# A decayed cumulative sum of a matmul: 210 of 264 slots ordered by a list scheduler, solved in place in a ring of seven tiles

## The chip, the cores and the metric

The kernel runs on one core of one Trainium2 chip. The metric is device microseconds of one execution. Engines are named as the profile names them: PE (TensorE matmul), PEld (its weight loads), DVE (VectorE), ACT (ScalarE), POOL (GpSimd), SP (SyncE, which here only issues stores).

## The reference

```python
B, S, D = 16, 2048, 1024
xw = x @ w                                    # x: [B, S, D], w: [D, D]
out[:, 0, :] = xw[:, 0, :]
for t in range(1, S):
    out[:, t, :] = decay[None, :] * out[:, t - 1, :] + xw[:, t, :]
```

Inputs and output are float32 in HBM. The kernel multiplies in bf16 and adds up in float32.

## The kernel before, in words

**Chunks and slots.** The 16 x 2048 rows of x are cut into 64 chunks of 512 rows. Two chunks of one batch entry are a group. For a group and one of eight blocks of 128 output columns PE makes one product of 128 columns by 1024 time steps, in a PSUM tile `ps` of which there are three. This is a *slot*: 16 matmuls of 128x512. There are 264 slots; the last group's two chunks are taken one at a time, in slots of half the size. Slot s of the middle of the kernel works on group s // 8, that is chunks 2(s // 8) and 2(s // 8) + 1, and on column block n = s % 8.

**How x comes in.** A chunk is loaded as four quads by POOL's DMA queue (`load`, letter L) into one of three `xb` tiles; DVE transposes it (`turn`, T) into one of two `xw` tiles; ACT copies it in two halves (`part`, X and Y) into one of five `xt` tiles, from which PE reads.

**How a slot is solved.** Most slots are *paired*. ACT copies the product to a tile `xs` (`copy`, p) and multiplies its even places by the decay into a tile `h` (`odd`, g); POOL adds these to the odd places (`join`, j); DVE scans only the odd places with the squared decay (`scan`, S) into a tile `so`; ACT multiplies the result by the decay again (`even`, h); POOL adds it to the even places (`fill`, c). ACT also copies the value before the first place (`zero`, z; POOL clears it at the start of a batch entry) and keeps the last one for the next group (`save`, k). A slot that is not paired is scanned whole by DVE, straight from PSUM. DVE then transposes `so` back (`back`, B) into an output tile `ot`. Four slots fill one `ot`, a *lump*; then SP issues four stores of 512 KB. Before, there are four `ot`, four `so`, three `xs`, four `h`. Of four slots three are paired, with a few exceptions listed in `flips`.

**What a release is.** PE may begin slot s when ACT (p and g) or, for a slot that is not paired, DVE (S) is done with `ps` of slot s - 3. A `so` is free again after its B, an `ot` after its four stores have landed, an `xt` after the last slot of its group, an `xb` after its T.

**What sets the order.** `pin` keeps each engine's instructions in the order in which the kernel's code issues them; an engine runs its list from the front, and an instruction that waits holds up what stands behind it. The text `agenda` gives the order slot by slot for slots 0 to 33 and for the last 20; for the slots between, `usual(s)` issues P, S, C, B in a fixed pattern, and `later` places each T, X and Y a fixed number of slots ahead of the group that needs it (11, 10 and 8 slots for an even chunk, 7, 6 and 4 for an odd one); one quad is loaded per slot.

In the built program the loads of x take eight semaphores in turn, and each load first waits until the load eight before it has landed.

Of the kernel before, what the change touches and what calls it, by code (L numbers as in the profile page):

```python
# [25 lines left out]
def kernel(  # L26
# [26 lines left out]
    nc = tc.nc  # L53
# [13 lines left out]
    CH = D // 2  # L67
    CR = CH // NQ

    const = ctx.enter_context(tc.tile_pool(name="const", bufs=1))  # L70
# [23 lines left out]
    def ot_tile(nj):  # L94
        return ring(sb, "ot", 4, [128, nj, CR])

# [22 lines left out]
    def part(c, copy, m0, m1, j0=0, j1=NJ):  # L119
        if c not in xt_of:  # L120
            xt_of[c] = ring(sb, "xt", 5, [128, M, 2, TL], BF16)
        src = xw_of[c][:, m0:m1, j0:j1].rearrange("p m j i e -> p m e (j i)")
        pin(copy(out=xt_of[c][:, m0:m1, :, j0 * P:j1 * P], in_=src))  # L123
# [17 lines left out]
    class Tile:  # L141
# [3 lines left out]
        def __init__(self, g, n, ps, outlets):  # L145
            self.b, self.t0 = chunks[g[0]]
            self.T = TL * len(g)
            self.n, self.ps, self.outlets = n, ps, outlets
            self.paired = n % R != R - 1
            if len(tiles) in flips or len(tiles) - len(slots) in flips:  # L150
                self.paired = not self.paired
            self.turn = len(tiles)
            self.lot = sum(t.paired for t in tiles)
            self.prev = None if self.t0 == 0 else last[n]
            if self.t0 + self.T < S:
                last[n] = const.tile([128, 1], FP32, name=f"keep{n}", bufs=2)
                self.keep = last[n]
            else:
                self.keep = None

        @property
        def so(self):
            if not hasattr(self, "held"):
                self.held = sb.tile([128, 2 * TL + 2], FP32, name=f"so{self.turn % 4}")
            return self.held

        def decayed(self, src):
            h = ring(sb, "h", 4, [128, TL])[:, 0:self.T // 2]
            pin(nc.scalar.activation(  # L169
                out=h, in_=src, func=mybir.ActivationFunctionType.Copy,  # L170
                scale=dec[:, self.n:self.n + 1]))
            return h
# [8 lines left out]
        def copy(self):  # L181
            self.xs = sb.tile([128, 2 * TL], FP32, name=f"xs{self.lot % 3}")[:, 0:self.T]
            pin(nc.scalar.copy(out=self.xs, in_=self.ps))  # L183

        def odd(self):
            self.g = self.decayed(self.ps[:, 0:self.T:2])

        def zero(self):
            if self.prev is None:
                pin(nc.gpsimd.memset(self.so[:, 1:2], 0.0))  # L190
# [3 lines left out]
        def join(self):  # L194
            odds = self.xs[:, 1:self.T:2]
            pin(nc.gpsimd.tensor_tensor(out=odds, in0=self.g, in1=odds, op=ALU.add))  # L196

        def scan(self):
            T, n, so = self.T, self.n, self.so
            if self.paired:  # L200
                pin(nc.vector.tensor_tensor_scan(  # L201
                    out=so[:, 3:T + 2:2],
                    data0=squares[-1][:, n:n + 1].to_broadcast([128, T // 2]),
                    data1=self.xs[:, 1:T:2],
                    initial=0.0 if self.prev is None else self.prev,
                    op0=ALU.mult,
# [8 lines left out]
        def run(self, ps, t, size):  # L215
# [3 lines left out]
            else:  # L219
                before = 0.0 if self.prev is None else self.prev  # L220
            pin(nc.vector.tensor_tensor_scan(  # L221
# [12 lines left out]
        def complete(self):  # L234
            if self.paired:
                self.even()
                self.fill()
            if self.keep is not None:
                self.save()

        def even(self):
            self.h = self.decayed(self.so[:, 1:self.T + 1:2])

        def fill(self):
            T = self.T
            pin(nc.gpsimd.tensor_tensor(  # L246
                out=self.so[:, 2:T + 2:2], in0=self.h, in1=self.xs[:, 0:T:2], op=ALU.add))

        def save(self):
            pin(nc.scalar.copy(out=self.keep, in_=self.so[:, self.T + 1:self.T + 2]))  # L250

# [14 lines left out]
    class Outlet:  # L266


        def __init__(self, ns, nj, half=0, queues=(nc.sync,), pieces=1):
            self.pieces = pieces  # L270
            self.ns, self.missing, self.half = ns, set(ns), half
            self.nj, self.t0, self.queues = nj, half * nj * P, queues
            self.ot = ot_tile(nj)

# [133 lines left out]
    def turn_and_load(c):  # L408
# [60 lines left out]
        20: "Y7 S19 L c16 k17 h17 T8 k19 L c17",  # L469
        21: "p20 g20 L S18 X8 j20 B17 B19",  # L470
        22: "L h18 p21 c18 B16 k18 g21 B18 Y8 z20 L j21 S20",
        23: "p22 z21 z22 S21 L h20 g22 T9 c20 h21",
        24: "k21 k20 j22 S23 X9 L c21 Y9 B20 L",
        25: "B23 k23 p24 B21 g24 z24 j24 S22 z25",
        26: "p25 T10 k22 h22 g25 c22 S24 X10 j25",
        27: "B22 p26 S25 g26 z26 Y10 j26",
        28: "S27 h25 h24 c25 S26 c24",
# [26 lines left out]
    flips = (1, 13, 15, -19, -18, -11, -8, -6, -3, -2)  # L504
    later = {}
    begun = {"T": 12, "X": 11, "Y": 11}
    for c in range(5, nch):
        first = c // 2 * K
        ahead = (7, 6, 4) if c % 2 else (11, 10, 8)
        for letter, a in zip("TXY", ahead):  # L510
            if c >= begun[letter]:
                later.setdefault(first - a, []).append(f"{letter}{c}")

    def usual(s):
        paired = [t.paired for t in tiles]
        do = [f"P{s}"] if paired[s] else []
        if paired[s - 1]:
            do.append(f"S{s - 1}")
        if not paired[s]:
            do.append(f"S{s}")  # L520
        do.append(f"C{s - 1}")
        if paired[s - 2]:
            do.append(f"B{s - 2}")
        if not paired[s - 1]:
            do.append(f"B{s - 1}")
        return do + later.get(s, []) + ["L"] * (2 if len(loads) > NQ else 1)

    def rest(s):
        do = [f"S{s - 1}"] if tiles[s - 1].paired else []
        do.append(f"C{s - 1}")  # L530
        if tiles[s - 2].paired:
            do.append(f"B{s - 2}")
        return do + [f"B{s - 1}"] + later.get(s, []) + ["L"] * len(loads)

    def perform(do):
        for deed in do:
            deeds[deed[0]](int(deed[1:] or 0))

    perform(agenda[-99].split())
    spares = [spare] + [ring(psp, "spare1", 1, [128, TL])]  # L540
    for step, (g, n) in enumerate(slots):
        T = TL * len(g)
        left = step - len(slots)
        if n % R == 0:
            ns, nj = range(n, n + R), T // P
            both = -6 * R <= left < -2 * R
            outlets = [Outlet(ns, nj, queues=(nc.sync, nc.gpsimd) if both else (nc.sync,),
                              pieces=2 if left == -2 * R else 1)]
        if left == -R:
# [52 lines left out]
        tiles.append(Tile(g, n, ps, outlets))  # L602
        do = agenda.get(step, agenda.get(left) if left >= -20 else None)
        if do is None:
            do = usual(step)
        else:
            do = do.split()
            if left == -20:
                do = rest(step) + do
        perform(do)  # L610
    assert not loads
# [28 lines left out]
```

## Time and profile before

| | us |
|---|---|
| Median of 3 runs (908.7 to 909.01) | 908.76 |
| Span of the profiled execution, first to last instruction | 907.2 |
| PE busy | 892.8 |
| DVE busy | 826.3 |
| ACT busy | 686.2 |
| POOL busy | 663.0 |

The profiled execution's own span is 907.2 us; the timed runs have 1.6 us more around it. Busy times count what overlaps on one engine once. PE's share cannot tell by itself whether PE could go faster, because its matmuls are pipelined and their ends are modelled; its list of waits and the number of weight loads in a stretch (one to a matmul) can. The trace lacks a few matmul records and the landing times of some stores.

### The profile page before, as it was taken

How to read it: one execution, taken by the hardware profiler on the slowest of the kernel's cores; microseconds unless marked ns; L12 is line 12 of the kernel's file. 1: busy time of each engine (PE TensorE's matmuls, PEld its weight loads, DVE VectorE, ACT ScalarE, POOL GpSimd, SP SyncE). 2: the span in 40 equal slices, each digit the busy share in tenths (PEclk: the TensorE clock that was granted, in tenths of full speed). 3: DMA queues.
4: the chain of work that ended last, by engine and by line, in shares of the span. 5: the costliest groups of instructions: out<-in, count | busy, mean ns of one | idle time of the engine just before them, and what ended most of it. 6: DMA issues, size and time to landing. Idle time of an engine off the chain costs nothing.

```text
span 907.2 us, 12004 instructions
## 1 busy us (share of the span) xinstructions
PE 892.8 (98%) x4119; PEld 411.4 (45%) x4201; DVE 826.3 (91%) x628; ACT 686.2 (76%) x955; POOL 663.0 (73%) x763
## 2 busy tenths in 40 slices
PE   9999999999999999999999999999999999999996
PEld 5444444444444444444444444444444444444443
DVE  4999989999999999899999999999999999999996
ACT  4889867777777877877877778778778778777742
POOL 7888678877777767768677777777677686776562
PEclk9999999999999999999999999999999999999999
DMA  9999999999999999999999999999999999999788
GB/s 194 194 215 220 227 215 220 215 238 255 249 250 254 241 243 259 247 244 228 227 233 227 227 232 227 226 232 233 220 230 231 228 231 223 232 229 207 153 161 211
DMA packets 397230, 204.77 MB, mean 226 GB/s; under 512 B 8816, under 2 KB 395376, under 8 KB 397168
## 3 DMA queue, kind: packets, MB, share of 16 engines
q1 hardware_dynamic: 258960, 131.62, 59.6%
q0 software_dynamic: 137920, 71.85, 58.1%
q8 instruction: 33, 0.54, 0.2%
q10 hardware_dynamic: 288, 0.52, 0.2%
q14 instruction: 29, 0.24, 0.1%
HBM read 138.42 MB, written 134.22 MB: 301 GB/s over the span
## 4 chain that ended last, share of the span: by engine, by line
PE 93%; DMA 2%; POOL 1%; issue 1%; DVE 1%; ACT 0%; POOLq 0%; DVEq 0%
PE ps L131 93%; DMA xb<-in_x_dram 2%; POOL ot L299 1%; POOL xb L105 1%; PE spare L131 1%; DVE xw L115 0%; ACT xt L123 0%; ACT xs L183 0%; DVE so L201 0%; PE spare L387 0%; DVE ot L258 0%; ACT h L169 0%; PE ps L387 0%; POOLq L635 0%; POOL xs L196 0%
## 5 line engine op out<-in xcount | busy, mean ns | idle before, releaser
L131 PE MATMUL ps<-xt,wsb 128*128 128x512 bf16 x3942 | 863.5, 378 | 4.7 <-ACT h L169 0.2
L131 PEld LDWEIGHTS <-wsb 128*128 128x128 bf16 x4152 | 405.9, 98 | 479.9 <-ACT wsb L306 0.8
L196 POOL TENSOR_TENSOR xs<-h,xs 128x512 f32<-128x512 f32 (+1 forms) x190 | 243.0, 1279 | 181.8 <-ACT h L169 79.4
L183 ACT COPY xs<-ps 128x1024 f32<-128x1024 f32 (+1 forms) x190 | 189.4, 997 | 155.3 <-PE ps L131 144.2
L258 DVE STREAM_TRANSPOSE ot<-so 128x1024 f32<-128x1024 f32 (+1 forms) x260 | 300.1, 1191 | 2.1 <-POOL so L190 1.1
L246 POOL TENSOR_TENSOR so<-h,xs 128x512 f32<-128x512 f32 (+1 forms) x190 | 241.4, 1272 | 39.0 <-ACT h L169 25.7
L123 ACT COPY xt<-xw 128x2048 bf16<-128x2048 bf16 (+1 forms) x136 | 242.3, 1790 | 7.8 <-DVE xw L115 7.6
L105 POOL DMA_DIRECT2D xb<-in_x_dram x264 | 174.3, 661 | 3.3 <-DMA ot<-in_w_dram 1.1
L169 ACT ACTIVATE h<-so,dec 128x512 f32<-128x512 f32 (+1 forms) x190 | 145.4, 766 | 27.7 <-DVE so L201 24.4
L115 DVE STREAM_TRANSPOSE xw<-xb 128x2048 f32<-128x2048 f32 (+1 forms) x78 | 147.4, 1901 | 5.5 <-DMA xb<-in_x_dram 5.5
L201 DVE TENSOR_TENSOR_SCAN so<-spare,keep,xs 128x512 f32<-128x512 f32 (+1 forms) x97 | 120.0, 1239 | 27.7 <-POOL xs L196 27.4
L201 DVE TENSOR_TENSOR_SCAN so<-spare,xs 128x512 f32<-128x512 f32 x93 | 113.3, 1220 | 27.6 <-POOL xs L196 24.6
L169 ACT ACTIVATE h<-ps,dec 128x512 f32<-128x512 f32 (+1 forms) x190 | 130.3, 686 | 0.0
L221 DVE TENSOR_TENSOR_SCAN so<-dec,ps 128x1024 f32<-128x1024 f32 x34 | 76.8, 2261 | 1.0 <-ACT h L169 1.0
L221 DVE TENSOR_TENSOR_SCAN so<-dec,keep,ps 128x1024 f32<-128x1024 f32 (+1 forms) x35 | 75.9, 2169 | 0.1
L250 ACT COPY keep<-so 128x1 f32<-128x1 f32 x136 | 25.3, 189 | 9.9 <-DVE so L221 9.4
L192 ACT COPY so<-keep 128x1 f32<-128x1 f32 x97 | 18.4, 191 | 2.6 <-DVE ot L258 2.4
L131 PE MATMUL ps<-xw,wsb 128*128 128x256 bf16 (+1 forms) x68 | 11.2, 301 | 0.1
L190 POOL MEMSET so<- 128x1 f32 x93 | 10.7, 117 | 0.6 <-DVE ot L258 0.6
L131 PE MATMUL spare<-xt,wsb 128*128 128x512 bf16 (+1 forms) x48 | 10.0, 335 | 0.0
L282 POOL DMA_DIRECT2D out_dram<-ot x8 | 5.7, 722 | 5.5 <-DVE ot L258 5.1
L299 POOL DMA_DIRECT2D ot<-in_w_dram x12 | 6.6, 546 | 3.3 <-DMA xb<-in_x_dram 2.0
(38 smaller groups left out, 44.5 us busy)
## 6 DMA issues: line engine op xcount, KB each, us to landing
out_dram<-ot SPq DMA_DIRECT2D x244, 512.0 KB, 10.9
xb<-in_x_dram POOLq DMA_DIRECT2D x248, 256.0 KB, 7.8
xb<-in_x_dram POOLq DMA_DIRECT2D x16, 128.0 KB, 5.8
out_dram<-ot POOLq DMA_DIRECT2D x4, 512.0 KB, 11.6
ot<-in_w_dram POOLq DMA_DIRECT2D x12, 128.0 KB, 5.1
out_dram<-ot SPq DMA_DIRECT2D x4, 256.0 KB
out_dram<-ot POOLq DMA_DIRECT2D x4, 256.0 KB, 8.5
out_dram<-ot SPq DMA_DIRECT2D x8, 128.0 KB, 4.3
```

The costliest lines, as they stand in the source:

```text
L105: pin(nc.gpsimd.dma_start(out=xb_of[c][quad(q), j0:j1], in_=_ap(x, [[D, P], [P * D, j1 - j0], [1, CQ]], (b * S + t0 + j0 * P) * D + q * CQ)))
L115: pin(nc.vector.transpose(out=dst.rearrange("p (m j i) -> p j m i", m=M, i=P)[:, j0:j1, m0:m1], in_=src.rearrange("p (j m c) -> p j m c", ...
L123: pin(copy(out=xt_of[c][:, m0:m1, :, j0 * P:j1 * P], in_=src))
L131: pin(nc.tensor.matmul(out=ps[:, t0:t1] if ps.shape[1] >= t1 else ps, lhsT=lhs, rhs=rhs, start=(k == 0 and t0 == start), stop=(k == K - 1),))
L169: pin(nc.scalar.activation(out=h, in_=src, func=mybir.ActivationFunctionType.Copy, scale=dec[:, self.n:self.n + 1]))
L183: pin(nc.scalar.copy(out=self.xs, in_=self.ps))
L196: pin(nc.gpsimd.tensor_tensor(out=odds, in0=self.g, in1=odds, op=ALU.add))
L201: pin(nc.vector.tensor_tensor_scan(out=so[:, 3:T + 2:2], data0=squares[-1][:, n:n + 1].to_broadcast([128, T // 2]), data1=self.xs[:, 1:T:2 ...
L221: pin(nc.vector.tensor_tensor_scan(out=so[:, t + 2:t + 2 + size], data0=dec[:, n:n + 1].to_broadcast([128, size]), data1=ps, initial=befor ...
L246: pin(nc.gpsimd.tensor_tensor(out=self.so[:, 2:T + 2:2], in0=self.h, in1=self.xs[:, 0:T:2], op=ALU.add))
L250: pin(nc.scalar.copy(out=self.keep, in_=self.so[:, self.T + 1:self.T + 2]))
L258: pin(nc.vector.transpose(out=outlet.ot[:, :, c0:c0 + P], in_=self.so[:, 2 + t0:2 + t0 + nj * P].rearrange("p (i t) -> p i t", t=P)))
```

## The change

The change replaces `usual` and `later`. For slots 34 to 243 a list scheduler in the kernel (`steady`, `in_order`) makes a job of each instruction, or of four matmuls for PE, with an engine, a cost in us, a due time (`key`) and the jobs that it comes after. It steps through time; an engine that is idle takes the ready job with the earliest due time, whatever that due time is. The order in which jobs start is the order in which they are issued. A load is assumed landed 9 us after its end (`LAND`), a store 13 us after the lump's last B (`STORED`). Chunks 12 to 14 have some or all of their quads loaded by the agenda; only quads still to be loaded become jobs.

Beside that:

- a product is copied straight into its `so` and solved there in place; `xs` is gone, and `so` has seven tiles, taken in turn at the copy;
- `ot` has three tiles instead of four, `xt` four instead of five; an `ot` is now taken when its first B is issued;
- which slots are not paired in 34 to 243 is set by a running sum (0.18 to a slot): 37 of 210, where it was 53;
- T is issued in two halves there;
- in the agenda X8 and Y8 move from slots 21 and 22 to 24, X9 and Y9 from 24 to 25 and 26, and X10 and Y10 leave it for the scheduler;
- code that merges the products of a group (`mixed_group`, `differ` and others) is added, but `merged` is empty and none of it runs.

```diff
+    OTS, XTS, SOS, HS = 3, 4, 7, 4
+    FROM, TO = 34, 244
+    SHARE = {-1: 0.08, 0: 0, 1: 0.12, 2: 0.16, 3: 0.18, 9: 0.18}
+    merged = ()
...
-        return ring(sb, "ot", 4, [128, nj, CR])
+        return ring(sb, "ot", OTS, [128, nj, CR])
...
-            xt_of[c] = ring(sb, "xt", 5, [128, M, 2, TL], BF16)
+            xt_of[c] = ring(sb, "xt", XTS, [128, M, 2, TL], BF16)
...
-                self.held = sb.tile([128, 2 * TL + 2], FP32, name=f"so{self.turn % 4}")
+                self.held = sb.tile([128, 2 * TL + 2], FP32, name=f"so{self.turn % SOS}")
...
         def copy(self):
-            self.xs = sb.tile([128, 2 * TL], FP32, name=f"xs{self.lot % 3}")[:, 0:self.T]
-            pin(nc.scalar.copy(out=self.xs, in_=self.ps))
+            pin(nc.scalar.copy(out=self.line, in_=self.ps))
...
         def join(self):
-            odds = self.xs[:, 1:self.T:2]
+            odds = self.line[:, 1:self.T:2]
             pin(nc.gpsimd.tensor_tensor(out=odds, in0=self.g, in1=odds, op=ALU.add))
...
-        21: "p20 g20 L S18 X8 j20 B17 B19",
-        22: "L h18 p21 c18 B16 k18 g21 B18 Y8 z20 L j21 S20",
+        21: "p20 g20 L S18 j20 B17 B19",
+        22: "L h18 p21 c18 B16 k18 g21 B18 z20 L j21 S20",
         23: "p22 z21 z22 S21 L h20 g22 T9 c20 h21",
-        24: "k21 k20 j22 S23 X9 L c21 Y9 B20 L",
-        25: "B23 k23 p24 B21 g24 z24 j24 S22 z25",
-        26: "p25 T10 k22 h22 g25 c22 S24 X10 j25",
-        27: "B22 p26 S25 g26 z26 Y10 j26",
+        24: "X8 k21 k20 j22 S23 Y8 L c21 B20 L",
+        25: "B23 k23 p24 B21 g24 z24 j24 S22 X9 z25",
+        26: "p25 T10 k22 h22 g25 c22 Y9 S24 j25",
+        27: "B22 p26 S25 g26 z26 j26",
...
+    def in_order():
...
+            for e, queue in ready.items():
+                if idle[e] > now:
+                    continue
...
+                job = heapq.heappop(queue)[2] if queue else None
...
+                order.append(job)
+                job.start = now
+                end = idle[e] = now + job.cost
...
+                for other, delay in next_to[job]:
+                    begin[other] = max(begin[other], end + delay + (GAP if other.engine != e else 0))
...
+    LAND = 9.0
+    STORED = 13.0
+    PASS = 0.2158
...
+        def chunk(c):
+            need = starts[c // 2] - 18 + (c % 2) * 5
+            if c > 11:
+                quads = [q for cc, q in loads if cc == c] if c <= 14 else range(NQ)
+                got = [Job("pool", cost["L"], need - 28 + 2.5 * q, lambda c=c, q=q: load(c, q),
+                           [turned.get(c - 3)]) for q in quads]
+                ends = [(a, LAND) for a in got]
+                for half in range(2):
+                    turned[c] = Job(
+                        "dve", cost["T"], need + 2 * half,
+                        lambda c=c, h=half: turn(c, 0, NJ, h * M // 2, (h + 1) * M // 2),
+                        ends + [turned.get(c - 1), part_of.get((c - 2, 1)), turned.get(c)])
+                    part_of[c, half] = Job(
+                        "act", cost["X"], need + 3 + 3 * half,
+                        lambda c=c, h=half: part(c, nc.scalar.copy, h * M // 2, (h + 1) * M // 2),
+                        [turned[c], part_of.get((c - 1, half))] + used.get(c - XTS, []))
...
+        def back(tile, end, key):
+            s = tile.turn
+            lump = s // R
+            first = firsts.get(lump - 1)
+            b = Job("dve", cost["B"], key + 6, tile.back,
+                    [end, place.get((s, "k"))] + stored.get(lump - OTS, []) + ([first] if first else []))
+            firsts.setdefault(lump, b)
+            place[s, "B"] = b
+            lumps.setdefault(lump, []).append((b, STORED))
+            if len(lumps[lump]) == R:
+                stored[lump] = lumps[lump]
...
+        order = in_order()
+        for job in order:
+            job.do()
...
     for step, (g, n) in enumerate(slots):
+        if FROM <= step < TO:
+            if step == FROM:
+                steady(outlets)
+            continue
...
-        do = agenda.get(step, agenda.get(left) if left >= -20 else None)
-        if do is None:
-            do = usual(step)
-        else:
-            do = do.split()
-            if left == -20:
-                do = rest(step) + do
-        perform(do)
+        perform(agenda.get(step, agenda.get(left)).split())
```

In the built program the first instructions of the scheduler's part stand like this (a number is the slot or the chunk, a small letter an instruction of a slot, as above). DVE: S33, B32, B33, both halves of T12, S34, S35, B34, S36, T13, B35, T13, B36, S37, S38, S39. POOL: the four L13, the first L14, c33, three L14, z34, j34, two L15, z35, one L15, j35, c34, z36, j36, one L15, c35. ACT: X10, k33, h33, X10, p34, g34, X11, p35, g35, h34, k34, p36, g36, X11, h35, k35, p37, h36, k36, g37. Slot 39 is not paired. The agenda's last loads, all four of chunk 12, stand two behind j32 and two behind c32 on POOL, before as after.

## The prediction

> **What bounds the kernel now.** I read the page first: its busy shares and its chain that ended last.
>
> ```profile
> span 907.2 us, 12004 instructions
> ...
> PE 892.8 (98%) x4119; PEld 411.4 (45%) x4201; DVE 826.3 (91%) x628; ACT 686.2 (76%) x955; POOL 663.0 (73%) x763
> ...
> PE ps L131 93%; DMA xb<-in_x_dram 2%; POOL ot L299 1%; POOL xb L105 1%; PE spare L131 1%; DVE xw L115 0%; ACT xt L123 0%; ACT xs L183 0%; DVE so L201 0%; PE spare L387 0%; DVE ot L258 0%; ACT h L169 0%; PE ps L387 0%; POOLq L635 0%; POOL xs L196 0%
> ```
>
> The chain is PE. Whether PE has gaps is told by its list of waits and by busy time in stretches of the middle.
>
> ```profile
> PE ps L131 <- ACT h L169: 0.2, 1, 0.2
> ...
> 200.00:300.00 100.00, 99.53 (x456) 45.33 (x464) 92.64 (x65) 77.52 (x106) 74.35 (x81) 1.00 1.23 251
> ```
>
> PE waits for another engine's `ps` release once, 0.2 us. In 100 us there are 464 weight loads, one to a matmul: 0.2155 us each, 3.45 us a slot, at a clock of 1.00. So PE runs without a gap through the slots that the change touches. The matmuls stay what they are, so this middle cannot become faster; the question is whether the new order keeps PE fed. Next I read who is close to being late: DVE around slot 34, the loads that it waits for, and the stores.
>
> ```profile
> 130.15 1.01 ACT L183 COPY xs<-ps 128x1024 f32<-128x1024 f32 x1 [1.09 <-PE ps L131]
> 134.58 1.30 POOL L105 DMA_DIRECT2D xb<-in_x_dram  x2
> 145.72 2.31 DVE L115 STREAM_TRANSPOSE xw<-xb 128x2048 f32<-128x2048 f32 x1 [0.56 <-DMA xb<-in_x_dram]
> ```
>
> From the timelines of ACT, POOL and DVE. The copy at 130.15 is that of slot 33, so slot 34 begins at 130.1 and slot s at 130.1 + 3.45 (s - 34). The last two quads of chunk 12 are issued at 134.6 and 135.2, and T12 waits for them until 145.7. That costs nothing now: it stands behind all that is due sooner.
>
> ```profile
> L282 SPq DMA_DIRECT2D out_dram<-ot x4: 4670/4723/4727, 156.9 to 171.1; - x4
> ...
> DMA to landing us min/median/max: 18.1/18.3/18.4
> ...
> L258 DVE STREAM_TRANSPOSE ot<-so x4: 1203/1212/1246, 134.7 to 142.9; 128x1024 f32<-128x1024 f32 x4
> L258 DVE STREAM_TRANSPOSE ot<-so x1: 1247/1247/1247, 175.9 to 175.9; 128x1024 f32<-128x1024 f32 x1
> L258 DVE STREAM_TRANSPOSE ot<-so x1: 1247/1247/1247, 189.7 to 189.7; 128x1024 f32<-128x1024 f32 x1
> ```
>
> From the instructions of `out_dram` and of line 258. 32 stores and 32 B precede, so these are lump 8 (slots 32 to 35): B done at 144.1, stores issued only from 156.9, the last landed at 171.1 + 18.4 = 189.5. The stores queue. With four `ot`, lump 12 takes this tile, first B at 189.7: 0.2 us to spare. Lump 11 begins at 175.9.
>
> **The change part by part.**
>
> *More paired slots.* 53 unpaired become 37, so 16 slots move. Rows by form: ACT p 1.012, g 0.694, h 0.775 and half a z of 0.19; POOL j 1.299, c 1.292; DVE one scan of 1.25 for one of 2.29. ACT gains 16 x 2.58 = 41 us, POOL 16 x 2.59 = 41, DVE loses 16 x 1.04 = 17. T in halves: a transpose of 128x1024 is 1.216, two are 0.15 more than the 2.285 of the whole, 52 times 8 us. Over the 725 us of the 210 slots busy shares go from 92 to 91% (DVE), 78 to 84 (ACT), 75 to 80 (POOL). None passes PE's 100: no cost by load, and DVE, which is nearest, gets a little looser. If a stall elsewhere makes DVE late, this cover is thin: it recovers some 9% of the time that passes.
>
> *Seven `so`, no `xs`, in place.* Same operations, sizes and strides; p now waits for the B of seven slots before (24 us) where it waited for a c of three paired slots before. No row shows a loss; 0, between -0.4 (below, last rival) and 0.
>
> *Four `xt`.* X may begin when the group before last ends, 27.6 us ahead; X8 to Y9 move to slots 24 to 26, needed at slot 32, at least 15 us ahead by the order. 0; ACT, which waits for chunk 8's place, does 3.8 us less in slots 21 and 22 and as much more in 24 to 26.
>
> *T12's place.* The scheduler has no load job for chunk 12, since the agenda issued them, so T12 counts as ready when X10 is done. DVE, idle until S34, takes it although it is due later. On the chip DVE runs its list in order and blocks on T12 till the data is there. First stall, slot 39, which needs slot 36's `ps`, released by g36, behind h34 and p36 on ACT:
> T12's data 145.7, as now, or up to 2.4 later, since its last quads stand behind c32 and DVE runs late there (next part); I take 147.0. Two halves 2.4 -> 149.4; S34 1.22 -> 150.6; h34 0.78, k34 0.19, p36 1.01, g36 0.69 -> 153.3. Slot 39 is due at 147.4. **5.9 us**, 4.6 with the data at 145.7.
> Second, slot 40, which needs g37, behind h35 and h36. On POOL j35 stands behind three loads of chunk 15. They need T12's tile, and by the eight semaphores the third waits for the third load of chunk 13, which landed at 153.2 before (issued 141.0, 12.2 on its way). It is now issued some 4 us sooner into the same queue: as low as 147 at 9.7 on its way (the median around there), as high as 153.2; I take 153.2, since the loads before it land no sooner. Then load 0.66, j35 1.30 -> 155.2. c34 1.29, z36 0.12, j36 1.30 -> 157.9; S36 1.22, h36 0.78, k36 0.19, g37 0.69 -> 160.8. Slot 40 is due at 153.3 + 3.45 = 156.8. **4.0 us**, 1.7 at the low end (j35 2.5 us sooner, when T12 alone holds the loads back).
> Third, slot 42, which needs S39, the unpaired slot. DVE after S36: T13 2.4, B35 and B36 2.4, S37 and S38 2.5, S39 2.3 -> 159.1 + 9.6 = 168.7, due at 160.8 + 6.9 = 167.7: **1.0**, between 0 and 2.
> After that DVE's list holds no transposes of loads from the agenda, and each quad is a job with 9 us to land; T stands tens of us behind its loads. I count nothing more, 0 to 3.
>
> *Three `ot`.* Lump 11's first B now waits for lump 8's landing: 189.5 against 175.9 now, 13.6 late, and as DVE blocks, PE stalls. By the order it is B45, some 2 us later than B44 was; S46 behind it, h46, p48, g48: 189.5 + 1.2 + 1.2 + 0.8 + 1.0 + 0.7 = 194.4, for slot 51 due at 188.8. Alone, 5.6 us; lumps 12 to 14 wait too and might make it 8. But a PE that is already 10.9 late has slot 51 due at 199.7. So the two stalls do not add up: the larger counts. Before slot 34: lump 5's first B at 99.1 waits for lump 2 (84.3 + 18.4 = 102.7), 3.6 us on a DVE that is 100% busy from 60 to 85 us. PE has `ps` to spare there by about as much: D27's release, now 111.7, goes to 115.3, slot 30 is due at 116.3. 0 for PE, at most 3.6; its mark is the lateness that I gave to T12's data. From about lump 18 the stores land in time for three tiles.
>
> *The sum.* 5.9 + 4.0 + 1.0 = 10.9 on this execution's 907.2: span 918.1; the median of the runs is 1.6 above the span: **919.7 us**.
>
> *The clock.* The row first: the granted clock is 1.00 from the first matmul, though the 22 spin matmuls take 0.43 each for 5 us, and 0.50 in the trace's last 2.7 us, from 5.5 us after PE's last work.
>
> ```profile
> 904.30:907.00 2.70, 0.00 (x0) 0.00 (x0) 0.00 (x0) 0.00 (x0) 0.00 (x0) 0.50 0.21 77
> ```
>
> The Trainium skill, "TensorE: Matmul & The Clock Gate", Part 1: The HAM clock gate, has PE at half rate after one idle window of about 3.4 us, until a busy one. By that rule, stalls one and two would each halve the clock, and an estimate from its window is 1.7 us more for each; no stall of PE in this trace shows it.
> By rows alone a stall that trips the clock costs up to 5.2 us at half speed, that is 2.6 us. The only idle time seen to trip it was 5.5 us, which stall one just reaches and two does not. I take 0 and make the drop a rival.
>
> **Rivals.**
> *Half of it.* The data comes at 145.7, chunk 13 early, so 4.6 + 1.7 = 6.3, or the three `ot` alone, 5.6: 914 to 915. For it: DVE rows overlap by 0.1 us each, so full durations overstate. Against: the landing 153.2 is a row.
> *It adds up.* The stall at slot 39 pushes lump 8's B past SP's free moment at 156.9; loads in bursts take the stores' bandwidth; lumps 11 to 14 land late again and DVE, 9% loose, does not recover: 10.9 + 5.6 is 925.3, with 3.6 for lump 5 and two clock drops 934. For it: PE must then wait for DMA, and its queues are busy in 9 of 10 tenths throughout. Against: a PE behind by 11 us asks for fewer bytes.
> *The clock drops* in the first stall, or in both: 2.6 or 5.2 on top, 922.3 or 924.9. For it: the row of 0.50 above. Against: stall one is 4.6 if the data is not late. (The clock rule of the Trainium skill, "TensorE: Matmul & The Clock Gate", is on this rival's side.)
> *No stall reaches PE* (the waits end within the 6.9 us that a `ps` has to spare): 908.8. It needs T12's data about 5 us sooner. Against: the quads' place in POOL's list has not changed.
> *Faster.* PE's gap before 47 us for h (0.2 in the row above), and the like at the end, close because p finds a free `so`: -0.4 us and no more, 908.4; with all of 1 us, 907.8. It decides only if no stall at all happens.
>
> **Chances and range.** The forecast with its own range of 917 to 922: 0.41. Half of it: 0.18. The clock drops: 0.13. It adds up: 0.20. No stall: 0.05. Faster: 0.03. Leaving out 2 in 10 at both ends: 913 to 931. A change of 0.2% (1.8 us) is about what a measurement here can tell from none; slower by more than that 0.92, within it 0.06, faster 0.02 (the gaps before 47 us hardly sum to it).
>
> **What would show it.** Right: in the changed profile a DVE wait of some 8 us for `xb` before T12 at about 146 to 148; PE waits for ACT at slots 39 and 40 of 4 to 6 us each; waits of line 273 (B) for stores at about 103 and 190; no PE gap after about 250 us; DVE below 92% there. Wrong: PE waits spread over the whole run, which would speak for the order itself being too tight; or a PE without gaps at 147; or loads of chunks 13 to 15 that never hold up POOL.

## The result and the profile after

The changed kernel takes 930.33 us (median of 4 runs, 929.61 to 934.66), the kernel before beside it 908.88 us (908.7 to 909.3): a ratio of 1.0245, 95% interval 1.0223 to 1.0267. It is slower by 21.5 us, where 10.9 us were forecast. The profiled execution's span is 929.2 us, 22.0 us more than before.

The page, then lines of the list of waits (engine and line, what it waited for, us in all, times, the longest), then the busy times in the same stretch as before (PE, PEld, DVE, ACT, POOL; clock, DMA, GB/s):

```profile
span 929.2 us, 11870 instructions
...
PE 897.7 (97%) x4119; PEld 412.2 (44%) x4201; DVE 804.9 (87%) x680; ACT 714.1 (77%) x1008; POOL 702.9 (76%) x806
```

```profile
DVE ot L273 <- DMA out_dram<-ot: 27.1, 10, 5.1
...
PE ps L138 <- ACT h L184: 14.2, 5, 7.0
```

```profile
200.00:300.00 100.00, 99.53 (x456) 45.30 (x463) 90.99 (x74) 83.59 (x115) 83.60 (x97) 1.00 1.21 222
```

No engine is fuller than PE: from 200 to 300 us PE still runs without a gap, DVE is at 91%, ACT and POOL at 84%. The loss is in a few places, and PE's list names them: five waits for ACT to release `ps`, 14.2 us, where there was one of 0.2 us. DVE's waits for stores before a B are 27.1 us. PE's timeline gives the places of the four long ones, at slots 37, 39, 40 and 106, and of a wait for DVE at slot 42 (slots 37, 39, 40, 42 and 106 begin in these five lines):

```profile
142.10 7.07 PE L138 MATMUL ps<-xt,wsb 128*128 128x512 bf16 x31 [1.84 <-ACT h L184]
156.14 5.56 PE L138 MATMUL ps<-xt,wsb 128*128 128x512 bf16 x16 [6.97 <-ACT h L184]
164.80 7.07 PE L138 MATMUL ps<-xt,wsb 128*128 128x512 bf16 x31 [3.10 <-ACT h L184]
172.25 2.97 PE L138 MATMUL ps<-xt,wsb 128*128 128x512 bf16 x13 [0.39 <-DVE so L236]
...
395.71 4.60 PE L138 MATMUL ps<-xt,wsb 128*128 128x512 bf16 x13 [2.14 <-ACT h L184]
```

The weight loads, one to a matmul, measure a gap more sharply than the modelled ends of matmuls: a step from one load to the next that is longer than 0.216 us is PE time lost. That gives this account, used for every run below:

| PE time lost, us | before | after |
|---|---|---|
| Opening: slots 37, 39, 40, 42 | 0 | 2.01 + 7.13 + 3.26 + 0.55 |
| Opening: matmuls at half clock | 0 | 1.94 |
| Middle: slot 106, half clock there, slot 231, one slow step | 0 | 2.30 + 1.63 + 0.54 + 0.15 |
| End: slots 248 and 249, the last transposes of PE | 0.4 | 1.54 + 0.46 + 1.78 |

The opening is 14.9 us, the middle 4.6, the end 3.4 more than before, of which 0.7 comes back because the span ends 7.5 us after PE's last transpose instead of 8.2. Slot 34 begins 0.15 us sooner: 14.9 + 4.6 + 2.7 - 0.15 = 22.0.

**The opening.** DVE's timeline, then POOL's:

```profile
144.66 1.25 DVE L273 STREAM_TRANSPOSE ot<-so 128x1024 f32<-128x1024 f32 x1 [5.87 <-POOL so L261]
150.24 2.37 DVE L122 STREAM_TRANSPOSE xw<-xb 128x1024 f32<-128x1024 f32 x2 [4.33 <-DMA xb<-in_x_dram]
152.54 1.19 DVE L216 TENSOR_TENSOR_SCAN so<-spare,so 128x512 f32<-128x512 f32 x1
159.53 1.22 DVE L216 TENSOR_TENSOR_SCAN so<-spare,so 128x512 f32<-128x512 f32 x1 [5.80 <-POOL so L211]
```

```profile
137.45 3.83 POOL L112 DMA_DIRECT2D xb<-in_x_dram  x6
142.67 0.64 POOL L112 DMA_DIRECT2D xb<-in_x_dram  x1 [1.39 <-DMA xb<-in_x_dram]
...
145.09 0.67 POOL L112 DMA_DIRECT2D xb<-in_x_dram  x1 [0.47 <-DMA xb<-in_x_dram]
147.57 0.65 POOL L112 DMA_DIRECT2D xb<-in_x_dram  x1 [1.82 <-DMA xb<-in_x_dram]
150.03 0.64 POOL L112 DMA_DIRECT2D xb<-in_x_dram  x1 [1.81 <-DMA xb<-in_x_dram]
...
150.72 1.30 POOL L211 TENSOR_TENSOR so<-h,so 128x512 f32<-128x512 f32 x1
152.94 0.67 POOL L112 DMA_DIRECT2D xb<-in_x_dram  x1 [0.91 <-DVE xw L122]
155.01 0.64 POOL L112 DMA_DIRECT2D xb<-in_x_dram  x1 [1.41 <-DMA xb<-in_x_dram]
...
157.53 0.64 POOL L112 DMA_DIRECT2D xb<-in_x_dram  x1 [1.77 <-DMA xb<-in_x_dram]
158.19 1.31 POOL L211 TENSOR_TENSOR so<-h,so 128x512 f32<-128x512 f32 x1
```

S34 (152.54) needs j34, and DVE has T12 ahead of it. T12 gets its data at 150.2. But j34, the add at 150.72, ends at 152.0 only, behind four loads of chunk 14, each of which waits until an earlier load has landed: they go out as loads land, one in about 2.45 us. So two different things hold S34 at almost the same moment, T12 and POOL's loads. S35 at 159.53 waits for POOL alone: j35 stands behind loads of chunk 15. But T12 acts here too, since the first of these loads (152.94) had to wait until T12 had freed its tile.

**The middle.** DVE's timeline before slot 106, the first B of lump 25:

```profile
390.94 1.25 DVE L273 STREAM_TRANSPOSE ot<-so 128x1024 f32<-128x1024 f32 x1 [5.08 <-DMA out_dram<-ot]
392.11 1.19 DVE L216 TENSOR_TENSOR_SCAN so<-spare,so 128x512 f32<-128x512 f32 x1
```

The B at 390.94 waits for the stores of lump 22, the tile's last user with three `ot`; the last of them landed at 390.8. The scan behind it on DVE starts 5 us late, and PE waits at 395.7. The profile's table of transfers says that all transfers have become slower, loads from 7.8 us to 10.6, stores from 10.9 to 12.3 (before, then after; the last column is the median time from issue to landing):

```profile
out_dram<-ot SPq DMA_DIRECT2D x244, 512.0 KB, 10.9
xb<-in_x_dram POOLq DMA_DIRECT2D x248, 256.0 KB, 7.8
```

```profile
out_dram<-ot SPq DMA_DIRECT2D x244, 512.0 KB, 12.3
xb<-in_x_dram POOLq DMA_DIRECT2D x248, 256.0 KB, 10.6
```

The scheduler's loads run further ahead. Counted from the issues, the loads before slot 106 are 6.5 chunks ahead of what the slot needs, 5.2 before; the stores issued are 2.5 lumps behind the slot, 1.2 before.

### The profile page after: what moved, and what is told of

It is laid out like the page before. It is cut to its first block, busy times and chain, and to the rows that moved or that the text cites. A ratio compares the mean times of both kernels' runs of the same rounds, so it can differ in the third digit from the quotient of the medians.

```text
span 929.2 us, 11870 instructions
## 1 busy us (share of the span) xinstructions
PE 897.7 (97%) x4119; PEld 412.2 (44%) x4201; DVE 804.9 (87%) x680; ACT 714.1 (77%) x1008; POOL 702.9 (76%) x806
## 4 chain that ended last, share of the span: by engine, by line
PE 60%; DMA 10%; DVE 8%; POOL 5%; issue 4%; SPq 2%; ACT 2%; DVEq 0%; POOLq 0%; ACTq 0%
PE ps L138 60%; DMA out_dram<-ot 6%; DMA xb<-in_x_dram 4%; DVE ot L273 3%; SPq L302 2%; DVE xw L122 2%; POOL so L211 2%; DVE so L216 2%; POOL so L261 2%; POOL xb L112 1%; DVE so L236 1%; ACT h L184 1%; ACT so L197 1%; POOL out_dram L302 0%; ACT xt L130 0%
## 5 line engine op out<-in xcount | busy, mean ns | idle before, releaser
L138 PE MATMUL ps<-xt,wsb 128*128 128x512 bf16 x3942 | 868.5, 379 | 21.3 <-ACT h L184 14.2
L273 DVE STREAM_TRANSPOSE ot<-so 128x1024 f32<-128x1024 f32 (+1 forms) x260 | 306.0, 1195 | 62.9 <-DMA out_dram<-ot 27.1
L261 POOL TENSOR_TENSOR so<-h,so 128x512 f32<-128x512 f32 (+1 forms) x206 | 262.9, 1282 | 124.4 <-ACT h L184 95.4
L211 POOL TENSOR_TENSOR so<-h,so 128x512 f32<-128x512 f32 (+1 forms) x206 | 264.0, 1283 | 54.8 <-ACT h L184 42.5
L197 ACT COPY so<-ps 128x1024 f32<-128x1024 f32 (+1 forms) x206 | 205.4, 997 | 69.0 <-PE ps L138 68.2
L184 ACT ACTIVATE h<-so,dec 128x512 f32<-128x512 f32 (+1 forms) x206 | 157.4, 766 | 99.9 <-DVE so L216 99.3
L122 DVE STREAM_TRANSPOSE xw<-xb 128x1024 f32<-128x1024 f32 (+2 forms) x130 | 152.4, 1194 | 10.0 <-DMA xb<-in_x_dram 9.2
L184 ACT ACTIVATE h<-ps,dec 128x512 f32<-128x512 f32 (+1 forms) x206 | 140.9, 684 | 0.0
L216 DVE TENSOR_TENSOR_SCAN so<-spare,so 128x512 f32<-128x512 f32 x104 | 124.6, 1204 | 16.7 <-POOL so L211 15.2
L216 DVE TENSOR_TENSOR_SCAN so<-spare,keep,so 128x512 f32<-128x512 f32 (+1 forms) x102 | 123.9, 1220 | 4.6 <-POOL so L211 4.3
L236 DVE TENSOR_TENSOR_SCAN so<-dec,keep,ps 128x1024 f32<-128x1024 f32 (+1 forms) x30 | 64.4, 2148 | 9.9 <-PE ps L138 8.7
L236 DVE TENSOR_TENSOR_SCAN so<-dec,ps 128x1024 f32<-128x1024 f32 x23 | 52.0, 2262 | 3.5 <-PE ps L138 3.4
## 6 DMA issues: line engine op xcount, KB each, us to landing
out_dram<-ot SPq DMA_DIRECT2D x244, 512.0 KB, 12.3
xb<-in_x_dram POOLq DMA_DIRECT2D x248, 256.0 KB, 10.6
```

Source lines behind the costliest of these rows:

```text
L122: pin(nc.vector.transpose(out=dst.rearrange("p (m j i) -> p j m i", m=M, i=P)[:, j0:j1, m0:m1], in_=src.rearrange("p (j m c) -> p j m c", ...
L138: pin(nc.tensor.matmul(out=ps[:, t0:t1] if ps.shape[1] >= t1 else ps, lhsT=lhs, rhs=rhs, start=(k == 0 and t0 == start), stop=(k == K - 1),))
L184: pin(nc.scalar.activation(out=h, in_=src, func=mybir.ActivationFunctionType.Copy, scale=dec[:, self.n:self.n + 1]))
L197: pin(nc.scalar.copy(out=self.line, in_=self.ps))
L216: pin(nc.vector.tensor_tensor_scan(out=so[:, 3:T + 2:2], data0=squares[-1][:, n:n + 1].to_broadcast([128, T // 2]), data1=so[:, 3:T + 2:2] ...
L236: pin(nc.vector.tensor_tensor_scan(out=so[:, t + 2:t + 2 + size], data0=dec[:, n:n + 1].to_broadcast([128, size]), data1=ps, initial=befor ...
```

## The experiments

The first theory was that of the prediction: T12's place and the loads around it make the opening's stall, and the third `ot` makes the rest, early on. Rivals put the opening on one cause alone, and slot 106 on what the opening left behind or on the later loads. Each run is one kernel with one or a few lines changed. Where no number of runs is given, it was timed once. The kernel before varied from 908.1 to 910.3 us, the changed one from 929.6 to 934.7, so what an edit does is read from PE's lost time in the trace, and a difference of a few us between times says little by itself. "Opening", "middle" and "end" are sums of lost PE time as in the table above (slots 34 to 44, 45 to 243, and from 244), half clock included.

| run | us | opening | middle | end |
|---|---|---|---|---|
| before | 908.9 | 0 | 0 | 0.4 |
| after | 930.3 | 14.9 | 4.6 | 3.8 |
| before, three `ot` | 914.05 | 0 | 4.9 | 1.2 |
| before, in place | 908.49 | 0 | 0 | 0.3 |
| after, four `ot` | 922.51 | 11.6 | 0 | 3.0 |
| after, T12 held back | 937.15 | 9.8 | 15.6 | 3.8 |
| after, loads spaced | 921.74 | 9.8 | 0 | 3.9 |
| after, both | 916.22 | 4.0 | 0 | 3.8 |
| after, T12 back, loads of chunks 13 to 15 spaced | 936.91 | 2.0 | 23.2 | 3.8 |
| after, loads from chunk 16 on spaced | 926.02 | 13.4 | 0 | 3.8 |
| after, both, four `ot` | 911.13 | 0 | 0 | 3.0 |
| the same, slot 243 not paired | 910.99 | 0 | 0 | 3.1 |
| the last, S243 behind S242 | 909.99 | 0 | 0 | 1.7 |
| before, three `ot`, loads in bursts | 923.23 | 5.6 | 7.7 | 1.9 |

**The third `ot`, taken out of the one kernel and put into the other.**

```diff
-        return ring(sb, "ot", 4, [128, nj, CR])
+        return ring(sb, "ot", 3, [128, nj, CR])
```

> The kernel before with one edit: three output tiles (ot) instead of four. Theory 1 (the stores' landing is a cause of its own): lump 11's first back-transpose waits for lump 8's stores until about 189.5 us, some 13 us after its place; PE stalls there by 6 to 9 us, and the clock may drop once for 1.7; lump 5's waits until about 102.5 and costs PE nothing: 915 to 920 us. Rival (three tiles matter only because the new order is late already): no PE gap over 1 us, 909 us.

914.05 us, a little under the theory's range and 5 us above the rival's value. Three `ot` alone cost the kernel before 0.54 us at slot 50, 2.69 at slot 54 and 1.68 at half clock; the first B of lumps 11 and 12 waits 3.47 and 4.16 us for stores. After that nothing: with the loads one to a slot, the stores do land in time for three tiles.

```diff
-    OTS, XTS, SOS, HS = 3, 4, 7, 4
+    OTS, XTS, SOS, HS = 4, 4, 7, 4
```

> The changed kernel with four output tiles again, nothing else undone. Theory 1 (causes are T12's place with the loads ahead of the joins, then the three tiles, then slot 243's chain at the end): no wait for stores at 102 and at 391 us, so the gap before slot 106 with its slow clock (3.9 us) and that before slot 37 (2.0) go; the gaps before slots 39 and 40 stay at 4 to 10 us together; the end keeps its 3.4: 917 to 923 us. Rival (the opening's stall is itself the three tiles' doing): the gaps before slots 39 and 40 go too, 912 to 914 us.

922.51 us, in the theory's range: 7.8 us less than the changed kernel. The stalls of the middle (slots 106 and 231) are gone, and so is slot 37's, which hence came from the third `ot`. The wait that it can have come from is that of lump 5's first B in the changed kernel:

```profile
102.22 3.50 DVE L273 STREAM_TRANSPOSE ot<-so 128x1024 f32<-128x1024 f32 x3 [3.40 <-POOL so L211]
```

The view puts this wait down to POOL, but the last store of lump 2, the tile's user before, landed at 102.10. How it leads to slot 37 was not traced further. Slots 39 and 40 stay, 4.50 and 3.22 us with 3.87 us at half clock. The last quads of chunk 12 are issued 3.1 us sooner than in the changed kernel, and T12 begins at 145.5 instead of 150.2.

**T12's place and the loads, one at a time and together.** T12 was held back by giving it a time before which it is not ready:

```diff
-                ends = [(a, LAND) for a in got]
+                ends = [(a, LAND) for a in got] or [(place[FROM - 1, "S"], 20)]
```

> The changed kernel, with the scheduler told that chunk 12 has landed only 20 us after slot 33's scan; T12 then stands behind slot 39's scan, and chunk 15's loads behind it, but the loads of chunk 14 still stand ahead of j34 on POOL. Theory 1 (T12 and the loads' semaphores each hold slot 34's scan till about 152 us): the gap before slot 39 stays at 5 to 7 us, with the clock's drop; that before slot 40 (3.3 us) goes; 925 to 928 us. Rival (T12 alone holds it): both gaps go and the clock stays up, 916 to 920 us.

937.15 us: worse than the change itself, and outside both ranges. The opening lost 9.8 instead of 14.9 us, but slot 39 still waited 6.58 us. T12 is no longer ahead of S34 in this kernel, and yet DVE's and POOL's timelines show S34 at almost the same time (152.54 before the edit):

```profile
151.85 2.50 DVE L216 TENSOR_TENSOR_SCAN so<-spare,so 128x512 f32<-128x512 f32 x2 [6.58 <-POOL so L205]
```

```profile
149.82 0.64 POOL L112 DMA_DIRECT2D xb<-in_x_dram  x1 [1.80 <-DMA xb<-in_x_dram]
...
150.51 1.30 POOL L211 TENSOR_TENSOR so<-h,so 128x512 f32<-128x512 f32 x1
```

The loads ahead of j34 are enough to hold it. The other way round, the loads were spaced in the scheduler's reckoning as the kernel before spaces them:

```diff
-                           [turned.get(c - 3)]) for q in quads]
+                           [turned.get(c - 3), (place[FROM - 1, "S"], 3 + 3.4 * (4 * (c - 13) + q))])
+                       for q in quads]
```

> The changed kernel with each load of the scheduler's part also held, in its reckoning, until 3.4 us after the load before it (as the kernel before spaces them, one to a slot); T12 stays where the change has it, ahead of S34. With T12 moved as well the time was 916.2. Theory 1 (T12's place costs by itself, as the prediction says): T12 waits for its data until about 145.5, S34 ends at 149, PE loses 2 to 3 us at slot 39 and perhaps 1.7 in a clock drop on top of what was left at 916.2: 918 to 921. Rival (the loads ahead of j34 and j35 are the whole of the opening stall, T12 none of it): 915.5 to 917.

921.74 us, above both ranges by a little: slot 39 lost 6.80 us and 1.32 in the clock, nothing else in opening and middle. Now the wait is T12's own, and its data is as late as in the changed kernel, 149.6 and not the 145.5 that I expected, as three `ot` are still there (its last quads were issued at 137.1):

```profile
149.59 2.37 DVE L122 STREAM_TRANSPOSE xw<-xb 128x1024 f32<-128x1024 f32 x2 [8.47 <-DMA xb<-in_x_dram]
```

With both edits:

> As the run with T12 held back, and each load from chunk 13 on may be issued only 3.4 us after the one before it. Theory 1: the gaps before slots 39 and 40 go, 12 us with the clock's drop; that before slot 37 stays at about 2. PE being early now, lump 11 waits for lump 8's stores and PE stalls around slot 51 by 4 to 8 us; the end keeps 3.4: 916 to 922 us. Rival (the order itself is too tight): gaps of 2 us and more stay in several places after 200 us, 923 us or more.

916.22 us, at the low end of the first theory's range: slots 39 and 40 are mended as it said, but the stall that it expected around slot 51 did not come. The four openings, 14.9, 9.8, 9.8 and 4.0, are the answer: either cause alone gives slot 39 nearly its full stall (6.58 and 6.80 us of 7.13), and only without both does it go. Slot 40's stall needs both causes together. This holds with three `ot`; T12's place alone with four, where its data comes at about 145.5, was not run. What is left, 2.30 us at slot 37 and 1.68 at half clock, goes with a fourth `ot`, as a run below shows.

**Where slot 106 comes from.** Holding back T12 made the middle worse (15.6 us). Two runs split the spacing at chunk 16. The first spaces only the opening's loads (with T12 held back):

```diff
+                           [turned.get(c - 3), (place[FROM - 1, "S"], 3 + 3.4 * (4 * (c - 13) + q))
+                            if c < 16 else None]) for q in quads]
```

> The changed kernel with T12 held back and only the loads of chunks 13 to 15 spaced by 3.4 us; from chunk 16 on the scheduler takes loads as early as it likes, as in the changed kernel. What it tells: where the stall at slot 106 comes from. Theory 1 (a backlog of stores carried along from the opening stall): no PE gap between slots 43 and 243, 916 to 917. Rival (the early loads of each later group take the stores' place in the DMA queues, whatever the opening was): PE gaps of 2 to 5 us each, with clock drops, at one or more slots from 60 to 231: 919 to 926.

The second leaves the opening as the change has it and spaces the rest:

```diff
+                           [turned.get(c - 3), (place[FROM - 1, "S"], 3 + 3.4 * (4 * (c - 13) + q))
+                            if c > 15 else None]) for q in quads]
```

> The changed kernel with its opening as it is, and the loads from chunk 16 on spaced by 3.4 us. Theory 1 (backlog carried from the opening): the stall at slot 106 stays or comes elsewhere, 928 to 931. Rival (early loads later on): opening 14 to 15 us and end 3.4 us stay, the 4.5 us of slots 106 and 231 go: 925 to 926.5.

936.91 and 926.02 us: the rival's side both times, the first beyond its range. With a good opening and early loads afterwards, the middle loses 23.2 us; with the bad opening and spaced loads, nothing. So a backlog from the opening does not make it. The early loads of each later group do, and only together with the third `ot`: with early loads and four `ot` (922.51 us), and with three `ot` and all loads spaced (916.22), the middle lost nothing. DVE's waits for stores in the first and in the second of these kernels:

```profile
DVE ot L273 <- DMA out_dram<-ot: 49.9, 16, 8.6
```

```profile
DVE ot L273 <- DMA out_dram<-ot: 3.4, 1, 3.4
```

And the opening's stall hid part of it: at slot 58 the stores issued are 1.8 lumps behind in the changed kernel, 3.0 behind where the opening was mended. A PE that is 15 us late had given the stores time.

**Early loads without a scheduler.** In the kernel before, with three `ot`, the loads of a chunk were issued together instead of one to a slot:

```diff
-        return do + later.get(s, []) + ["L"] * (2 if len(loads) > NQ else 1)
+        return do + later.get(s, []) + ["L"] * len(loads)
```

> The kernel before with three `ot` (914.05 alone) and the four loads of a chunk issued together as soon as they may be, rather than one to a slot. Its T's stay at their slots, so the loads cannot run further ahead than about a chunk. Theory 1 (stores are late whenever loads come early, by bursts too, and three `ot` show it to PE): gaps after slot 54 as well, 917 or more. Rival (bursts do no harm while the loads stay as far ahead as before; only the scheduler, which moves the T's forward too, gets them 6.5 chunks ahead): 913.5 to 915.5.

923.23 us: 9.2 more than with three `ot` alone, the first theory. Both mechanisms appear in an order that no scheduler made. POOL's loads hold a fill until 150.5, as in the changed kernel, and PE loses 3.72 us at slot 41, then 1.68 at half clock and 0.22 more. Later DVE waits for stores 38 times, against 4 times and 11.2 us with the loads one to a slot:

```profile
147.40 0.65 POOL L105 DMA_DIRECT2D xb<-in_x_dram  x1 [1.80 <-DMA xb<-in_x_dram]
149.87 0.64 POOL L105 DMA_DIRECT2D xb<-in_x_dram  x1 [1.81 <-DMA xb<-in_x_dram]
150.52 1.29 POOL L246 TENSOR_TENSOR so<-h,xs 128x512 f32<-128x512 f32 x1
```

```profile
DVE ot L258 <- DMA out_dram<-ot: 67.2, 38, 5.0
```

The loads are only 5.5 chunks ahead there, against 5.2. So a burst is enough; it needs hardly any greater distance. Why a burst slows the stores (their median here is 12.9 us from issue to landing, 10.3 in the run with three `ot` alone) I did not take further apart; that they share the DMA engines with the loads is argued, not shown.

**The tiles alone.** The kernel before, its order and buffers kept, solved in place in seven `so`:

```diff
-                self.held = sb.tile([128, 2 * TL + 2], FP32, name=f"so{self.turn % 4}")
+                self.held = sb.tile([128, 2 * TL + 2], FP32, name=f"so{self.turn % 7}")
...
-            self.xs = sb.tile([128, 2 * TL], FP32, name=f"xs{self.lot % 3}")[:, 0:self.T]
+            self.xs = self.so[:, 2:self.T + 2]
...
-                    data1=self.xs[:, 1:T:2],
+                    data1=so[:, 3:T + 2:2],
```

> The kernel before, its order kept, with the product copied straight into `so`, seven `so` and no `xs`: one part of the change alone. Theory of the order (the tiles cost nothing, as the prediction's step "Seven so, no xs, in place" has it): 908.5 to 909.3, PE's gaps as before. Rival (a copy that waits for the B of seven slots before is sometimes late, or work in place is dearer): PE gaps spread over the slots, 911 or more.

908.49 us beside 908.79, one run of each: no cost, and no gain that could be told.

**All three causes away, and the end.** Spaced loads, T12 held back and four `ot` together:

> The changed kernel with T12 held back, all loads of the scheduler's part spaced by 3.4 us, and four `ot`. Theory (early loads, T12's place and the third `ot` are together the whole loss before slot 244): no PE gap from slot 34 to 243, the 2.5 to 3 us at the end left: 911 to 912. Rival (the scheduler's order is too tight in itself, which the fourth `ot` does not cure): gaps left in the middle, 913 or more.

911.13 us (8 runs), 1.0029 of the kernel before, interval 1.0019 to 1.0040. There is no gap from slot 34 to 243. So the 37 unpaired slots, four `xt`, halved T's and the order of everything but loads and T12 cost PE nothing there. The end remains, and I took it to be slot 243, which the change pairs:

```diff
+    alone.add(TO - 1)
```

> The same, with slot 243 not paired, as in the kernel before, so that its chain of copy, join, scan and fill is off the path at the hand-over to the agenda. Theory (the end's loss comes from slot 243 being paired): the gaps at slots 248, 249 and before the last transposes go, 908.5 to 909.3, the same as the kernel before. Rival (other slots near the hand-over, 241 and 242, hold up the transposes as well): 910 to 912.

910.99 us, 1.0028 (1.0018 to 1.0038): not the theory's time but the rival's, and the end lost 3.1 us as before. DVE's timeline shows why:

```profile
854.92 2.29 DVE L236 TENSOR_TENSOR_SCAN so<-dec,ps 128x1024 f32<-128x1024 f32 x1 [3.74 <-PE ps L138]
857.13 1.20 DVE L216 TENSOR_TENSOR_SCAN so<-spare,so 128x512 f32<-128x512 f32 x1
```

S243, now read straight from `ps`, stands ahead of S241 on DVE and waits 3.7 us for PE, while the join of slot 241 has been done since 853.2. It is T12's mistake again, with PE in place of a load. With slot 243 paired, as in the run before and in the changed kernel, S243 does stand behind S242; there the last B of lump 60 waits for slot 243's own fill instead. It ends at 864.1 us in the run before and at 864.0 in this one, against 861.6 in the kernel before (the line is of the run before):

```profile
862.85 1.25 DVE L273 STREAM_TRANSPOSE ot<-so 128x1024 f32<-128x1024 f32 x1 [0.94 <-POOL so L261]
```

In the last run slot 243 is not paired and S243 must come after S242:

```diff
-                end = pos("S", "dve", "D", 2, tile.scan, ready + [gone, prev])
+                end = pos("S", "dve", "D", 2, tile.scan, ready + [gone, prev]
+                          + ([place[s - 1, "S"]] if s == TO - 1 else []))
```

> As the run before it (T12 held back, loads spaced, four `ot`, slot 243 not paired), with the scan of slot 243 also made to come after that of slot 242. In the run before, DVE took the scan of slot 243 first, waited 3.7 us for PE, and the scans of 241 and 242, whose joins were done, stood behind it; lump 60 was finished 2.4 us later than in the kernel before, its two stores on POOL's queue stand ahead of the clear and the join of slot 244, and slots 246 and 247 were scanned 2.4 us late. Theory (this order at the hand-over is the loss at the end): the gaps at slots 248 and 249 shrink from 2.1 us to 1 or less, 908.8 to 910. Rival (lump 60 comes late by other waits as well): 910.5 to 911.5.

909.99 us (10 runs), 1.0013 (1.0004 to 1.0023). The gap at slot 248 shrank from 1.62 to 0.2 us; 0.45 at slot 249 and about 1 us before the last transposes stay, and their cause was not sought. So pairing slot 243 does cost at the end, 1.3 us by PE's account of this run and of the one with slot 243 paired; the theory fell only because taking the pairing away put S243 in a new wrong place. No run here is clearly faster than the kernel before: its PE has 0.4 us of gaps after 60 us, so there is little to win.

## Why the prediction was right in the opening and far too low in all

The direction, the place and the mechanism of the opening were as forecast: PE waits at slots 39, 40 and 42 for ACT and then DVE, behind T12 and behind loads on POOL. The sum was 10.9 us, the loss 22.0. The three stalls of the sum measured 10.94 together, but this agreement is luck, as none of the three is right by itself. What the sum lacks is 3.6 us at half clock, 2.0 at slot 37, 3.0 of waits in the middle and 2.7 at the end, less the 0.15 by which slot 34 begins sooner. By the prediction's steps:

- **"T12's place"**, first stall, 5.9 us: it measured 7.13, and 2.01 were lost before it at slot 37. What was mis-sized is the time at which T12 gets its data, taken as 147.0 and measured 150.2, beyond the range of 145.7 to 148.1 that was given. The cause was also only half named: slot 39 had two sufficient causes, T12 and the loads ahead of j34; the step counted the loads for j35 only. An edit to the named cause alone left 6.58 us of that stall standing.
- Its second stall, 4.0: 3.26. Third, 1.0: 0.55. j35 ended 4.3 us later than worked out (159.5 against 155.2), because the third load of chunk 13 landed at 157.25, not at 153.2, the latest time that was allowed. Slot 40 was due later as well, by 4.7 us (161.5 against 156.8), 1.9 of it by the half clock that was counted as nothing. So 3.26 lies near 4.0 because two errors cancel; at full clock the stall would have been 5.2 us, by an estimate from these times.
- **"The clock"**, taken as 0: 1.94 us in the opening and 1.63 at slot 106. It was rightly a rival, at 2.6 us; the runs measured 1.3 to 2.8 a drop. The one row of 5.5 us was a poor bound: a gap of 2.30 us halved the clock at slot 106. (Nor do the 22 spin matmuls take 0.43 us each: they fill 7.5 us, 0.34 each on average.) The rule of the Trainium skill, "TensorE: Matmul & The Clock Gate", Part 1: The HAM clock gate, is half rate after one idle window of about 3.4 us. The traces agree with that length, and the prediction's estimate from it, 1.7 us a drop, lies among the measured ones; they do not agree with a window idle throughout, as slot 106 halved the clock with 2.30 us. The second stall, which the prediction took to halve it by that rule, did not. The section on the hardware below gives the windows.
- **"Three `ot`"**, before slot 34: 0 was taken, up to 3.6 allowed. It is 2.0 at slot 37, as the run with four `ot` shows, and its lateness moved the last loads of chunk 12. For lump 11, "the larger counts" held: from 172 us until 379 us PE lost nothing. Alone it was put at 5.6 to 8, and three `ot` alone measured 5.
- **"From about lump 18 the stores land in time for three tiles"** and **"I count nothing more, 0 to 3"** are the steps that failed. They took the stores' times from the kernel before, whose loads go out one to a slot. That held in that kernel (no gap after slot 54 with three `ot`), but not under the new order of loads: 4.6 us in the middle, 1.6 of it at half clock. The rival "It adds up" named loads in bursts that take the stores' bandwidth, with 925.3 us and up to 934, and let it act on lumps 11 to 14. In its place the runs showed a loss at lump 25 (slot 106): lumps 11 to 14 cost PE nothing while PE was late by the opening (with the opening mended, slot 59 lost 8.2 us).
- The end was not looked at: 2.7 us of span, at the hand-over back to the agenda. By the last runs about half of it comes from pairing slot 243; the rest stays open.
- **"Seven `so`, no `xs`, in place"**, **"Four `xt`"**, **"More paired slots"**, all 0: right from slot 34 to 243, by the in-place run and by the middle without a gap in the last runs; for the paired slot 243 see the end.

Of the signs named beforehand, T12's wait for `xb` and B's wait at 102.2 came true, with T12's wait 4.3 us long and not 8, since DVE had stood 5.9 us behind POOL's loads first. DVE was below 92%, as named (91% from 200 to 300 us). There was no wait for stores near 190. "No PE gap after about 250 us" was wrong.

## What to carry to other kernels

When the order of work is drawn anew, draw the transfers' times anew too: how long a store takes was a property of the spacing of the loads, and a buffer fewer was free only while that spacing lasted. A list that always takes what is ready has no reason to hold back, but on an engine that runs its list in order a load or a transpose issued early stops everything behind it; give such work an earliest time, not only a due time. Two causes can each hold the same instruction: removing one and seeing little change does not acquit it, so remove both, and expect that a mended stall uncovers the next one (in its one run, the kernel with the opening alone mended was 6.6 us slower than the change).

## What the runs showed of the hardware that was not expected

The granted clock changes only at times that lie whole multiples of 3.413 us apart. In the changed kernel's trace it fell at 153.29, rose at 160.11, fell at 395.63 and rose at 399.05 us, which is 2, 69 and 1 times 3.413; the other eight traces in which it falls give the same step. So I read it as judged in windows of that length that run on from one to the next, and a window need not be idle from end to end. Before slot 106 PE was idle 2.23 us of one by the weight loads (2.06 by the modelled ends of matmuls in this view), and the next ran at half speed (columns: the window, its length, PE busy, granted clock, DMA, GB/s):

```profile
392.22:395.63 3.41, 1.35 (x7) 1.00 1.30 215
395.63:399.04 3.41, 3.33 (x8) 0.50 1.15 332
399.04:402.45 3.41, 3.36 (x16) 1.00 0.94 230
```

Over nine traces, 13 windows between 60 and 900 us ended in a drop; PE was idle 2.23 to 3.41 us in them. At full clock, no window with up to 2.11 us of idle time did so. The 3.26 us at slot 40 fell 1.99 and 1.27 into two windows and cost no clock; what a gap costs depends on where it falls.

The second is the rate of loads when they queue. With loads and stores both waiting, ten loads of 256 KB landed from 142.4 to 164.5 us in the changed kernel, about 2.45 us apart. As a load had to wait for an earlier one to land, POOL, an engine 76% busy, stood for up to 1.8 us at a load.
